# A feed-forward stage of seven products per group: the product with the fourth weight quarter goes second, and is kept in SBUF

## The chip, the cores and the metric

The kernel runs on one core of a Trainium2 chip. The metric is the device time of one execution, in microseconds (us). Inside the core, TensorE (PE) multiplies matrices and writes PSUM; VectorE (DVE) and ScalarE (ACT) work elementwise; GpSimd (POOL) does a few small operations and issues DMAs that add to their target; SyncE (SP) issues all other DMAs of weights. Every engine works through its own instructions in a fixed order, and waits for the others through semaphores.

## The reference

Two layers of an encoder trunk, 512 tokens by 1024 features, float32. A layer is an attention and pooling stage, with a residual, and then a gated feed-forward stage with a residual:

```python
hn = rmsnorm(x, norm2_g[i])
gate, up = jnp.split(hn @ w_ffn_in[i], 2, axis=-1)
x = x + (jax.nn.silu(gate) * up) @ w_ffn_out[i]
```

`w_ffn_in` is 1024 x 5632, `w_ffn_out` is 2816 x 1024. The change is in the feed-forward stage, and in a few buffers that it borrows from the attention stage.

## The kernel before

**Splitting.** TensorE multiplies in a format with fewer bits than float32, so each float32 operand is split into a high part (`whi`, `xh`, `fh`) and a low part (`wlo`, `xl`, `fl`), and a product is three matmuls (`three`, L279): high by high, high by low, low by high. A weight piece is 128 x 1024 floats, 0.5 MB. It is loaded by SP into one of seven buffers `raw` (`loaded`, L219) and split into one of six pairs of buffers `whi` and `wlo` (`parts`, L229), in one of two ways. Without a piece number ACT casts the high part and DVE subtracts for the low part (L212). With a piece number ACT casts the high part (L236), ACT writes its negative into `wlo` (L237), and POOL issues a DMA that loads the same piece from HBM once more and adds it to `wlo` (L238): this is called the correction below.

**Feed-forward.** The 22 blocks of 128 hidden features are worked in six parts. Two blocks, the odd group (`odd_group`, L820), are multiplied in the plain way. The other twenty form five groups of four (`GROUPS`, L40), and in each group the product of tokens by weights is computed in the way of Strassen and Winograd: the input is cut in four quarters (two halves of the tokens, two halves of the 1024 features) and so is the weight (two halves of the features, two pairs of hidden blocks), and seven products of quarters or of sums of quarters take the place of eight. They are numbered 1 to 7. Products 1, 2 and 4 use weight quarters as loaded; 5, 6, 7 and 3 use sums and differences that DVE makes in place in the `raw` buffers (L887, L893, L894, L907). The sums of the input are made once in a layer (`Sets`, L712; `sums`, `third`, `fourth`).

A product is 24 matmuls of 128 x 128 by 128 x 512 (two weight pieces, two token blocks of 128, two feature blocks, three matmuls each) into two PSUM banks, one for each token block. The banks come from three small pools: `sc` (2 banks, `a`), `tr` (2 banks, `c`) and `mm` (3 banks, `b`, shared with other work).

The order of the products is written out by hand:

```python
PRODUCTS = (1, 5, 6, 2, 7, 4, 3)
LOADS = {1: ((0, 0),), 5: ((1, 0), (1, 4)), 2: ((0, 4),), 4: ((1, 4),)}
```

`LOADS` says which quarters (pair of blocks, first feature block) are loaded ahead of a product, each as two pieces. The fourth quarter, (1, 4), is loaded twice in a group: for the first sum (product 5) and again for product 4 as a plain quarter. The first sum is built in the buffer of the fourth quarter, the second sum in the buffer of the first quarter, which so stays held until product 3.

After product 1 its result is copied to SBUF (`x1`, L925), and product 2 goes on adding to the same banks; the sum goes to `put`. Product 7 adds to the banks of product 6, once DVE has read them for `x2` (L933). After 7, DVE makes `x1` (L943) and `c22` (L945), reading banks `b` and `c`; after 4 it makes the last sum (L954); product 3 adds to banks `c` (L957) and ends `x2` (L959).

**Hidden blocks.** `put` (L797) applies the gate (ACT, L804, and DVE, L805) and turns the block by tokens into one by features: DVE transposes 32 x 32 squares (L316), SP stores the block to HBM (`away`, L317) and loads it back in another order with four DMAs (`near`, L321). `back` (L813) then splits it into `fh` and `fl` (L212).

**Output units.** A unit (`out_unit`, L836) multiplies 128 output features with the hidden blocks of one group into a bank, in turn `oy` or one of `mm`, and DVE adds it to the residual (L707). Units of an earlier group are put between the products of a later one by the table `UNITS` (L43): the key is the group and the product after which they stand. The last eight pairs of units follow after the fifth group.

**What sets the order.** The order on PE is fixed as written (`in_turn`, L288, ties each chain of matmuls to the one before it). On the other engines and on SP's queue, a scheduler orders the instructions at compile time by their place in the program and by when it reckons them ready; at run time each engine keeps that order. `later` (L260) puts the second half of a turn further on in the program.

**Borrowed buffers.** `rotate` (L368) uses two small tiles `m1` and `m2`, with two buffers each. The head gains of the two layers have a tile each (`hg0`, `hg1`, L188), and the row of norms of a layer lies in the tile of the other layer (L482). The pool weights' two parts have a tile each (L651).

## Time and profile before

| what | value |
|---|---|
| three runs | 1403.54, 1403.58, 1405.05 us |
| median of the runs | 1403.58 us |
| the profiled execution | 1406.57 us |
| its span, first to last instruction | 1404.8 us |
| granted TensorE clock, mean | 0.996 |
| weight loads `raw<-in_wts` issued by SP | 264 of 512 KB, 4.6 us to landing (median) |
| corrections `wlo<-in_wts` issued by POOL | 64 of 512 KB, 7.9 us to landing (median) |

The profile comes from one execution, 3.0 us longer than the median of the runs. In a row of its timeline stand the start, the duration (or, for merged instructions, the whole stretch), the engine, the line, the operation with its target and sources, the shapes and the count; in square brackets the engine's idle time before it, and what ended that. "SPq" is SP's queue of DMA issues. In a row of a table by windows stand the window, its length, and for PE, weight loads, DVE, ACT and POOL the busy time with the number of instructions that touch the window; then the granted clock, the share of the 16 DMA engines' time that packets took, and GB/s. Busy matmuls overlap, so that PE's busy time can be full while it runs slowly; the number of matmuls in a window of given length shows that.

### The profile page before, as it was taken

The numbers are of one execution on the slowest core, as the hardware profiler recorded it, in microseconds if no ns is written. First come the engines' busy times: TensorE is split into PE (matmuls) and PEld (weight loads), VectorE is DVE, ScalarE is ACT, GpSimd is POOL, SyncE is SP. The second block draws the span as 40 slices with busy tenths as digits, with TensorE's granted clock in tenths as the row PEclk, the third lists the DMA queues.
The fourth block names the chain that finished last, engine by engine and source line by source line (L and its number), as shares of the span: only waits on it lengthen the run. The fifth ranks groups of instructions, "written<-read, shape, count | busy, mean of one in ns | idle before, by whom it ended". The sixth has DMA issues, their size and how long they took to land.

```text
span 1404.8 us, 18608 instructions
## 1 busy us (share of the span) xinstructions
PE 1380.7 (98%) x6242; PEld 1140.8 (81%) x6242; DVE 1046.0 (74%) x1979; ACT 694.7 (49%) x1301; POOL 117.7 (8%) x139
## 2 busy tenths in 40 slices
PE   9999999999999999999999999999999989999999
PEld 7888888887887788888878787888878867888887
DVE  7779788686877768587667886877868767686772
ACT  7445343444765455545345543445457644555450
POOL 1010000000111000100010101001001100001000
PEclk9999999999999999999999999999999999999999
DMA  8334454455496876878434345534534967869661
GB/s 304 106 128 121 142 150 142 130 146 145 91 253 156 257 208 195 219 194 264 128 110 136 108 143 182 160 122 127 174 106 96 271 162 236 232 174 242 193 178 60
DMA packets 143663, 235.00 MB, mean 167 GB/s; under 512 B 41168, under 2 KB 88784, under 8 KB 143568
## 3 DMA queue, kind: packets, MB, share of 16 engines
q1 hardware_dynamic: 133056, 198.14, 43.2%
q0 software_dynamic: 9216, 33.56, 13.5%
q10 hardware_dynamic: 1296, 2.12, 0.5%
q8 instruction: 49, 0.80, 0.2%
q14 instruction: 46, 0.38, 0.1%
HBM read 204.53 MB, written 29.23 MB: 166 GB/s over the span
## 4 chain that ended last, share of the span: by engine, by line
PE 84%; DMA 6%; DVE 5%; issue 2%; ACT 1%; POOL 1%; SPq 1%; ACTq 0%; POOLq 0%; DVEq 0%
PE mm L301 12%; PE mm L302 12%; PE mm L303 12%; PE mm L283 6%; PE mm L284 6%; PE mm L282 6%; PE sc L283 3%; PE sc L282 3%; PE sc L284 3%; PE oy L282 3%; PE oy L284 3%; PE oy L283 3%; PE tr L282 2%; PE tr L283 2%; PE tr L284 2%; DMA away<-near 2%
## 5 line engine op out<-in xcount | busy, mean ns | idle before, releaser
L212 ACT CAST whi<-raw 128x1024 fp32r<-128x1024 f32 (+1 forms) x241 | 251.1, 1048 | 207.6 <-PE mm L283 53.5
L212 DVE TENSOR_TENSOR wlo<-raw,whi 128x1024 fp32r<-128x1024 f32 (+1 forms) x241 | 291.3, 1213 | 62.5 <-ACT whi L212 61.5
L301 PE MATMUL mm<-whi,xh 128*128 128x512 f32 x480 | 188.7, 393 | 1.0 <-DVE qn L601 1.0
L303 PE MATMUL mm<-whi,xl 128*128 128x512 f32 x480 | 187.2, 390 | 0.0
L302 PE MATMUL mm<-wlo,xh 128*128 128x512 f32 x480 | 187.1, 390 | 0.0
L303 PEld LDWEIGHTS mm<-whi,xl 128*128 128x128 f32 x480 | 90.1, 188 | 19.1
L301 PEld LDWEIGHTS mm<-whi,xh 128*128 128x128 f32 x480 | 90.2, 188 | 18.6 <-PE mm L303 1.4
L302 PEld LDWEIGHTS mm<-wlo,xh 128*128 128x128 f32 x480 | 90.2, 188 | 17.4
L238 POOL DMA_DIRECT2D wlo<-in_wts x64 | 56.1, 876 | 565.6 <-ACT wlo L237 390.3
L346 POOL TENSOR_TENSOR r<-r,mhalf 128x1 f32<-128x1 f32 (+1 forms) x64 | 56.7, 887 | 525.8 <-DVE r L345 422.8
L301 PE MATMUL mm<-xh,whi 128*128 128x512 f32 x256 | 99.8, 390 | 0.0
L302 PE MATMUL mm<-xl,whi 128*128 128x512 f32 x256 | 99.7, 390 | 0.0
L303 PE MATMUL mm<-xh,wlo 128*128 128x512 f32 x256 | 99.6, 389 | 0.0
L283 PE MATMUL sc<-wlo,xh 128*128 128x512 f32 x240 | 94.2, 393 | 5.5 <-DMA wlo<-in_wts 5.5
L707 DVE TENSOR_TENSOR res<-mm,res 128x512 f32<-128x512 f32 x96 | 65.2, 681 | 39.8 <-PE mm L284 33.6
L282 PE MATMUL sc<-whi,xh 128*128 128x512 f32 x240 | 94.1, 392 | 0.0
L284 PE MATMUL sc<-whi,xl 128*128 128x512 f32 x240 | 94.1, 392 | 0.0
L237 ACT ACTIVATE wlo<-raw 128x1024 fp32r<-128x1024 f32 x64 | 67.4, 1057 | 23.1 <-PE mm L283 14.0
L282 PE MATMUL oy<-fh,whi 128*128 128x512 f32 (+1 forms) x180 | 69.9, 388 | 6.1 <-DVE res L707 6.1
L284 PE MATMUL oy<-fh,wlo 128*128 128x512 f32 (+1 forms) x180 | 69.8, 388 | 0.0
L283 PE MATMUL oy<-fl,whi 128*128 128x512 f32 (+1 forms) x180 | 69.7, 387 | 0.0
L282 PE MATMUL mm<-fh,whi 128*128 128x512 f32 (+1 forms) x176 | 68.5, 389 | 0.0
(239 smaller groups left out, 3100.7 us busy)
## 6 DMA issues: line engine op xcount, KB each, us to landing
raw<-in_wts SPq DMA_DIRECT2D x264, 512.0 KB, 4.6
wlo<-in_wts POOLq DMA_DIRECT2D x64, 512.0 KB, 7.9
away<-near SPq DMA_DIRECT2D x72, 256.0 KB, 2.6
near<-away SPq DMA_DIRECT2D x288, 64.0 KB, 2.1
away<-near SPq DMA_DIRECT2D x28, 128.0 KB, 1.7
near<-away SPq DMA_DIRECT2D x112, 32.0 KB, 2.6
res<-in_x_t SPq DMA_DIRECT2D x4, 512.0 KB, 6.8
pwr<-in_pool_w ACTq DMA_DIRECT2D x8, 256.0 KB, 2.7
```

The costliest lines, as they stand in the source:

```text
L212: return nc.scalar.copy(hi, src), nc.vector.tensor_sub(lo, src, hi.bitcast(F32))
L237: made[0] = nc.scalar.activation(lo, raw, AF.Copy, scale=-1.0)
L238: nc.gpsimd.dma_start(lo.rearrange("p a b -> p (a b)"), wts[piece_no], accum_op=ALU.add)
L282: nc.tensor.matmul(acc, lhsT=ah, rhs=bh, start=start, stop=False, **check)
L283: nc.tensor.matmul(acc, lhsT=ah, rhs=bl, start=False, stop=False, **check)
L284: last = nc.tensor.matmul(acc, lhsT=al, rhs=bh, start=False, stop=stop, **check)
L301: nc.tensor.matmul(acc, lhsT=ah, rhs=bh, start=i == 0, stop=False)
L302: nc.tensor.matmul(acc, lhsT=ah, rhs=bl, start=False, stop=False)
L303: last = nc.tensor.matmul(acc, lhsT=al, rhs=bh, start=False, stop=i == n - 1)
L346: nc.gpsimd.tensor_tensor(r, r, mhalf[:, :width], op=ALU.pow)
L707: return nc.vector.tensor_add(res[d][:, cs], acc, res[d][:, cs])
```

## The change

Product 4 moves from the sixth place to the second. The fourth quarter is loaded once: its two pieces are split for product 4 by casts and correction, and the same `raw` buffers then serve the first sum. Product 4's result is copied from PSUM into SBUF by ACT (`x4`) and added, in SBUF, to `x1` after product 7, where both halves of the second pair of blocks are then put. The second sum has tiles of its own, under the tags `pw` and `hg`, where the pool weights' two parts now share one tile, and where one tile holds the head gains and the row of norms, for both layers in turn. `m1` and `m2` become parts of one tile with one buffer, which also holds one half of `x4`. `UNITS` is written for the new order; the units keep their places in the sequence. `third` is called after product 5 instead of 6, and `fourth` before the groups instead of at product 7.

```diff
-PRODUCTS = (1, 5, 6, 2, 7, 4, 3)
-LOADS = {1: ((0, 0),), 5: ((1, 0), (1, 4)), 2: ((0, 4),), 4: ((1, 4),)}
-UNITS = {(0, 7): [(-1, 0)], (0, 4): [(-1, 1)], (0, 3): [(-1, 2)], (1, 1): [(-1, 3)], (1, 4): [(0, 0)], (1, 3): [(0, 1)],
-         (2, 1): [(0, 2)], (2, 5): [(0, 3)], (2, 4): [(1, 0)], (2, 3): [(1, 1)],
-         (3, 1): [(1, 2)], (3, 5): [(1, 3)], (3, 4): [(2, 0)], (3, 3): [(2, 1)],
-         (4, 1): [(2, 2)], (4, 5): [(2, 3)]}
+PRODUCTS = (1, 4, 5, 6, 2, 7, 3)
+LOADS = {1: (0, 0), 4: (1, 4), 5: (1, 0), 2: (0, 4)}
+UNITS = {(0, 2): [(-1, 0)], (0, 7): [(-1, 1)], (0, 3): [(-1, 2)], (1, 1): [(-1, 3)],
+         (1, 7): [(0, 0)], (1, 3): [(0, 1)], (2, 1): [(0, 2)], (2, 4): [(0, 3)],
+         (2, 7): [(1, 0)], (2, 3): [(1, 1)], (3, 1): [(1, 2)], (3, 4): [(1, 3)],
+         (3, 7): [(2, 0)], (3, 3): [(2, 1)], (4, 1): [(2, 2)], (4, 4): [(2, 3)]}
...
-    for tag in ("m1", "m2"):
-        sb.tile([P, 4, ROT], F32, name=tag, tag=tag, bufs=2)
+    sb.tile([P, 4, 4, ROT], F32, name="m12", tag="m12")
...
-        g = sb.tile([P, 2 * QK + VD], F32, name="hg", tag=f"hg{layer}")
-        qkg[layer], sg[layer] = g[:, :2 * QK], g[:, 2 * QK:]
+        g = sb.tile([P, 2, S], F32, name="hg", tag="hg")
+        qkg[layer], sg[layer], rms_rows[layer] = g[:, 0, :2 * QK], g[:, 0, 2 * QK:], g[:, 1, :]
...
-            hi = sb.tile([P, 2, VD], F32R, name="pwh", tag="pwh")
-            lo = sb.tile([P, 2, VD], F32R, name="pwl", tag="pwl")
+            both = sb.tile([P, 2, 2, VD], F32R, name="pw", tag="pw")
+            hi, lo = both[:, 0], both[:, 1]
...
                 if not k:
                     x.sums()
+            x.fourth()
             token_stats(False)
```

The new `prepare` and the new loop over the products:

```python
def prepare(n):
    got = [loaded() for _ in range(2 if n in LOADS else 0)]
    if got:
        raws[n] = [raw for raw, _ in got]
    if n in (1, 4, 2):
        sets[n] = [parts(*r) for r in got]
        return
    sets[n] = []
    for h in range(2):
        if n == 5:
            made_of = raws[4][h]
            with ExitStack() if g else tc.issue_after(x.added.ins):
                nc.vector.tensor_add(made_of, raws[5][h], made_of)
        elif n == 6:
            made_of = sb.tile([P, 2, 512], F32, name="s2", tag=("pw", "hg")[h])
            nc.vector.tensor_sub(made_of, raws[4][h], raws[1][h])
            nc.vector.tensor_sub(raws[5][h], raws[1][h], raws[5][h])
            raws.setdefault(6, []).append(made_of)
        elif n == 7:
            made_of = raws[5][h]
        else:
            made_of = raws[2][h]
            nc.vector.tensor_sub(made_of, made_of, raws[6][h])
        sets[n].append(parts(made_of))
...
for n in PRODUCTS:
    prepare(n)
    if n in (4, 6):
        b = [mm_ps() for _ in range(2)]
    bank = {1: a, 2: a, 4: b, 6: b, 7: b, 5: c, 3: c}[n]
    multiply(n, bank, n in (1, 4, 5, 6))
    for t in range(2):
        if n == 1:
            x1[t] = temp("ta", 2)
            nc.scalar.copy(x1[t], a[t])
        elif n == 4:
            x4[t] = temp(*(("qn", 3), ("m12",))[t])
            nc.scalar.copy(x4[t], b[t])
        elif n == 6:
            x2[t] = temp("qn", 3)
            nc.vector.tensor_add(x2[t], b[t], x1[t])
        elif n == 2:
            to[0].put(0, t, a[t][:, :VD], a[t][:, VD:])
        elif n == 7:
            nc.vector.tensor_add(x1[t], b[t], x1[t])
            c22 = temp(("ah", "al")[t])
            nc.vector.tensor_add(c22, c[t], x1[t])
            to[1].put(1, t, c22[:, :VD], c22[:, VD:])
        elif n == 3:
            nc.vector.tensor_add(x2[t], c[t], x2[t])
            to[0].put(1, t, x2[t][:, :VD], x2[t][:, VD:])
    if n == 7:
        for t in range(2):
            nc.vector.tensor_add(x4[t], x4[t], x1[t])
            to[1].put(0, t, x4[t][:, :VD], x4[t][:, VD:])
    if n == 5 and not g:
        x.third()
```

More of the change, by code (lines that the diff above doesn't have):

```diff
@@ L109, in weight_plan @@
             for n in PRODUCTS:
-                for q in LOADS.get(n, ()):
-                    for h in range(2):
-                        quarter(f0, *q, h)
+                for h in range(2 if n in LOADS else 0):
+                    quarter(f0, *LOADS[n], h)
                 for source, i in UNITS.get((g, n), ()):
@@ L370, in rotate @@
         ca = cos_t[:, t, :].unsqueeze(1).broadcast_to([P, 4, ROT])
-        m1 = sb.tile([P, 4, ROT], F32, name="m1", tag="m1", bufs=2)
-        m2 = sb.tile([P, 4, ROT], F32, name="m2", tag="m2", bufs=2)
+        both = sb.tile([P, 4, 4, ROT], F32, name="m12", tag="m12")
+        m1, m2 = both[:, 0], both[:, 1]
         nc.vector.tensor_mul(m1, qn[:, :, :ROT], ca)
@@ L474, in trunk_kernel @@
     head_gains(0)
-    rms_rows = {}
     def spread_rms(layer):
@@ L481, in spread_rms @@
             transpose(row[:, token(t)], stats[0][:, 1, t:t + 1].broadcast_to([P, P]))
-        rms_rows[layer] = sb.tile([P, S], F32, name="rr", tag=f"hg{1 - layer}")
         nc.scalar.copy(rms_rows[layer], row)
@@ new lines, in prepare @@
+                got = [loaded() for _ in range(2 if n in LOADS else 0)]
[3 more added lines that the diff above has]
+                    sets[n] = [parts(*r) for r in got]
+                    return
+                sets[n] = []
+                for h in range(2):
+                    if n == 5:
+                        made_of = raws[4][h]
+                        with ExitStack() if g else tc.issue_after(x.added.ins):
+                            nc.vector.tensor_add(made_of, raws[5][h], made_of)
+                    elif n == 6:
+                        made_of = sb.tile([P, 2, 512], F32, name="s2", tag=("pw", "hg")[h])
+                        nc.vector.tensor_sub(made_of, raws[4][h], raws[1][h])
+                        nc.vector.tensor_sub(raws[5][h], raws[1][h], raws[5][h])
+                        raws.setdefault(6, []).append(made_of)
+                    elif n == 7:
+                        made_of = raws[5][h]
+                    else:
+                        made_of = raws[2][h]
+                        nc.vector.tensor_sub(made_of, made_of, raws[6][h])
+                    sets[n].append(parts(made_of))
@@ L916, in multiply @@
                                 start and not h)
-            x1, x2, c22 = [None] * 2, [None] * 2, [None] * 2
+            x1, x2, x4 = [None] * 2, [None] * 2, [None] * 2
             for n in PRODUCTS:
                 prepare(n)
-                if n == 1:
-                    multiply(1, a)
-                    for t in range(2):
+                if n in (4, 6):
+                    b = [mm_ps() for _ in range(2)]
+                bank = {1: a, 2: a, 4: b, 6: b, 7: b, 5: c, 3: c}[n]
+                multiply(n, bank, n in (1, 4, 5, 6))
+                for t in range(2):
+                    if n == 1:
@@ L932, in group @@
                         x2[t] = temp("qn", 3)
                         nc.vector.tensor_add(x2[t], b[t], x1[t])
-                    if not g:
-                        x.third()
-                elif n == 2:
-                    multiply(2, a, False)
-                    for t in range(2):
+                    elif n == 2:
                         to[0].put(0, t, a[t][:, :VD], a[t][:, VD:])
-                elif n == 7:
-                    multiply(7, b, False)
-                    for t in range(2):
+                    elif n == 7:
@@ L943, in group @@
                         nc.vector.tensor_add(x1[t], b[t], x1[t])
-                        c22[t] = temp(("ah", "al")[t])
-                        nc.vector.tensor_add(c22[t], c[t], x1[t])
-                    if not g:
-                        x.fourth()
-                    for t in range(2):
-                        to[1].put(1, t, c22[t][:, :VD], c22[t][:, VD:])
-                elif n == 4:
-                    a = [s_ps() for _ in range(2)]
-                    multiply(4, a)
-                    for t in range(2):
-                        nc.vector.tensor_add(x1[t], a[t], x1[t])
-                        to[1].put(0, t, x1[t][:, :VD], x1[t][:, VD:])
-                elif n == 3:
-                    multiply(3, c, False)
-                    for t in range(2):
+                        c22 = temp(("ah", "al")[t])
@@ L959, in group @@
+                        nc.vector.tensor_add(c22, c[t], x1[t])
+                        to[1].put(1, t, c22[:, :VD], c22[:, VD:])
+                    elif n == 3:
                         nc.vector.tensor_add(x2[t], c[t], x2[t])
                         to[0].put(1, t, x2[t][:, :VD], x2[t][:, VD:])
+                if n == 7:
+                    for t in range(2):
+                        nc.vector.tensor_add(x4[t], x4[t], x1[t])
+                        to[1].put(0, t, x4[t][:, :VD], x4[t][:, VD:])
@@ L961, in group @@
+                if n == 5 and not g:
+                    x.third()
                 for source, i in UNITS.get((g, n), ()):
```

41 lines of the change are left out of this document (3 added, 38 removed).

## The prediction

> **What bounds the kernel now.** The page first: its head and its rows for the engines and the DMA queues.
>
> ```profile
> span 1404.8 us, 18608 instructions
> PE 1380.7 (98%) x6242; PEld 1140.8 (81%) x6242; DVE 1046.0 (74%) x1979; ACT 694.7 (49%) x1301; POOL 117.7 (8%) x139
> ...
> q1 hardware_dynamic: 133056, 198.14, 43.2%
> q0 software_dynamic: 9216, 33.56, 13.5%
> ```
>
> TensorE is the bound, and the change leaves each of its 6242 matmuls in place. Only time in which PE stands still or runs slowly can be won. The PE waits, by cause (total, times, longest):
>
> ```profile
> PE oy L282 <- DVE res L707: 6.1, 3, 2.2
> PE sc L283 <- DMA wlo<-in_wts: 5.5, 3, 2.0
> ```
>
> Both are feed-forward lines: L707 empties the bank `oy` of an output unit, and `wlo` from `in_wts` is the correction that POOL's DMA adds to a weight (L238). PE's timeline holds all six:
>
> ```profile
> 437.90 0.50 PE L282 MATMUL oy<-fh,whi 128*128 128x512 f32 x1 [2.16 <-DVE res L707]
> 458.60 0.47 PE L283 MATMUL sc<-wlo,xh 128*128 128x512 f32 x1 [2.05 <-DMA wlo<-in_wts]
> 1136.52 0.50 PE L282 MATMUL oy<-fh,whi 128*128 128x512 f32 x1 [2.04 <-DVE res L707]
> 1152.19 0.47 PE L283 MATMUL sc<-wlo,xh 128*128 128x512 f32 x1 [1.53 <-DMA wlo<-in_wts]
> 1157.08 0.47 PE L283 MATMUL sc<-wlo,xh 128*128 128x512 f32 x1 [1.88 <-DMA wlo<-in_wts]
> 1194.40 0.47 PE L282 MATMUL oy<-fh,whi 128*128 128x512 f32 x1 [1.93 <-DVE res L707]
> ```
>
> Together 11.59 us idle, all in the second group of a layer or at the third group's first unit. The whole loss shows when those stretches are set beside the undisturbed ones after them (windows: length, PE busy and matmuls, ..., granted clock, DMA share, GB/s):
>
> ```profile
> 430.00:490.00 60.00, 55.79 (x231) 44.97 (x230) 45.05 (x57) 32.39 (x41) 5.22 (x6) 0.94 0.73 203
> 490.00:550.00 60.00, 60.00 (x266) 49.71 (x265) 43.90 (x56) 31.93 (x40) 5.21 (x6) 1.00 0.77 214
> ...
> 1128.00:1200.00 72.00, 64.62 (x282) 52.27 (x281) 53.31 (x68) 36.40 (x47) 5.22 (x6) 1.00 0.67 191
> 1200.00:1272.00 72.00, 72.00 (x319) 59.63 (x318) 51.38 (x64) 38.13 (x45) 6.95 (x8) 1.00 0.78 215
> ```
>
> 60 us hold 265 intervals, 0.2265 us a matmul. 35 are missing in layer 0 (7.9 us) and 37 in layer 1 (8.4 us): **16.3 us** lost, 11.6 of it idle. Most of the rest is clock, in layer 0:
>
> ```profile
> 438.00:442.00 4.00, 4.00 (x12) 3.15 (x13) 3.97 (x5) 1.75 (x3) 0.00 (x0) 0.64 0.40 94
> ```
>
> Right after the 2.16 us stop the granted clock was 0.64 for 4 us (4 x 0.36 = 1.4 us). Over the 60 us it was 0.94 in layer 0, some 3 us lost, and 1.00 in layer 1. The Trainium skill, "TensorE: Matmul & The Clock Gate", section "Why this matters for your kernels", asks only that no gap passes about 3 us; by that rule these stops would cost no clock, and the saving below would be 11.6 us and the restarts. The row above speaks against it.
>
> **Why these stops.** The first one backwards (ACT, then DVE, then SP's queue):
>
> ```profile
> 431.51 0.62 ACT L212 CAST fh<-near 128x512 fp32r<-128x512 f32 x1 [7.47 <-DMA near<-away]
> ```
> ```profile
> 432.16 0.69 DVE L212 TENSOR_TENSOR fl<-near,fh 128x512 fp32r<-128x512 f32 x1 [6.41 <-ACT fh L212]
> ...
> 437.16 0.68 DVE L707 TENSOR_TENSOR res<-oy,res 128x512 f32<-128x512 f32 x1
> ```
> ```profile
> 418.40 0.38 SPq L317 DMA_DIRECT2D away<-near  x1
> ...
> 423.81 2.66 SPq L321 DMA_DIRECT2D near<-away  x4
> ```
>
> A hidden block, turned through HBM, left at 418.40 and was back only at 431.5. ACT and DVE, both in order, held still for it, and the emptying of `oy` stood behind. The turn was slow because the DMA engines were full (windows; the last two numbers are DMA share and GB/s):
>
> ```profile
> 372.00:392.00 20.00, 20.00 (x94) 16.67 (x93) 15.45 (x26) 11.27 (x16) 1.97 (x2) 1.00 0.27 84
> 392.00:428.00 36.00, 36.00 (x160) 29.80 (x160) 25.34 (x34) 19.60 (x25) 4.35 (x5) 1.00 1.02 268
> ...
> 490.00:526.00 36.00, 36.00 (x160) 29.84 (x159) 23.25 (x27) 18.89 (x23) 3.49 (x4) 1.00 0.77 210
> ```
>
> The second stop, at 458.60, follows from the raw buffers (SP's waits, then DVE, SP, POOL):
>
> ```profile
> SPq L224 <- DVE raw L894: 50.3, 8, 19.3
> ```
> ```profile
> 442.48 1.22 DVE L894 TENSOR_TENSOR raw<-raw 128x1024 f32<-128x1024 f32 x1
> ```
> ```profile
> 443.76 17.68 SPq L224 DMA_DIRECT2D raw<-in_wts  x8
> ```
> ```profile
> 449.51 0.88 POOL L238 DMA_DIRECT2D wlo<-in_wts  x1 [1.03 <-ACT wlo L237]
> ```
>
> All seven raw buffers were held until L894, which DVE reached late for the reason above; product 2's second piece was loaded at 443.76, corrected from 449.51, and came in at 458.5.
>
> **The change, part by part.**
>
> *Two loads fewer in a group*, 20 of 0.52 MB. By the q1 row (607 us for 198.14 MB) one takes 1.6 us of all 16 engines; a correction, by the q0 row (190 us for 64), 3.0 us.
>
> *Buffers come free sooner.* Before, product 6 frees the two buffers of the first sum, and six stay held until 7 and 3: the pieces of 1 (as second sum), of 5 and of 2. After, the second sum has its own tiles, 6 frees the pieces of both 1 and 4, and four stay. So I expect that the output piece, the next one and a piece of the next group load before 392, where the share is 0.27, and that product 4's two corrections leave there too, instead of at 405:
>
> ```profile
> 390.41 0.93 POOL L238 DMA_DIRECT2D wlo<-in_wts  x1 [5.19 <-ACT wlo L237]
> ...
> 405.08 1.89 POOL L238 DMA_DIRECT2D wlo<-in_wts  x2 [11.43 <-ACT wlo L237]
> ```
>
> Out of the stretch 392 to 428 go 2 x 1.6 (dropped) + 3 x 1.6 (earlier) + 2 x 3.0 = 14 us; back come the next group's two corrections for product 4, 6 us. 36.7 - 8 = 29 us of 36: share 0.8, about that of 490 to 526, where nothing stops. I take all six stops as gone; the ends are none (0) and all (16.3 us).
>
> *Product 2 now has its weight slots from product 4*, with 5 and 6 between, as it had 1's slots with 5 and 6 between in the first group. First use there and the landing times:
>
> ```profile
> 400.45 0.39 PE L283 MATMUL sc<-wlo,xh 128*128 128x512 f32 x1
> ```
> ```profile
> DMA to landing us min/median/max: 5.4/7.9/10.8
> ```
> ```profile
> L925 ACT COPY cta<-sc 128x512 f32<-128x512 f32 x20 | 11.4, 586 | 5.4 <-PE sc L284 5.3
> ```
>
> That was 10.0 us from issue to use, without a stop. Afterwards two more copies (product 4 into SBUF, 0.59 each) stand on ACT before the second piece's casts; I work out 11.8 and 10.7 us of lead. The median fits; the largest misses the second by 0.1. Taken as 0; the price if the lead is used up is a rival below.
>
> *The copies* add 20 x 0.59 = 11.7 us to ACT (49% busy), beside PE; product 6 needs their `mm` banks one product, 5.4 us, later. The final add reads SBUF instead of PSUM: one add for one add. 0, or, if ACT is held as at 431.51, 2 us in a group.
>
> *Product 3 moves up behind 7.* It accumulates on bank `c`, which the add into `c22` must have read. In groups 1 to 4 a unit stands between; in the fifth none does, where now product 4 (5.4 us) does (DVE, then PE):
>
> ```profile
> 647.46 1.28 DVE L943 TENSOR_TENSOR cta<-mm,cta 128x512 f32<-128x512 f32 x2
> 648.66 0.68 DVE L945 TENSOR_TENSOR cah<-tr,cta 128x512 f32<-128x512 f32 x1
> ```
> ```profile
> 647.53 0.39 PE L284 MATMUL mm<-whi,xrl 128*128 128x512 f32 x1
> 647.75 0.39 PE L282 MATMUL sc<-whi,xh 128*128 128x512 f32 x1
> ```
>
> Product 3 would start at 647.75, and `c` is read at 649.34: **a new stop** of 1.6 us, 1.85 with restart, once in each layer: 3.7 us. It is 0.2 if DVE adds straight away in order, 2.9 if one more 1.2 us weight split goes first; 0.4 to 5.8 for both. I take the row as it stands. Behind this matmul stands all the rest of the layer on PE, so the stop counts in full.
>
> *Merged tiles.* `m1`/`m2` in one single buffer: all on DVE, in order, 0. The second layer's gains share a tile with the sums, and so can load only when the last group has let go, not here:
>
> ```profile
> 337.48 0.38 SPq L190 DMA_DIRECT2D hg<-in_rows  x1
> ```
>
> It would wait on SP, with raw loads behind it, until the fifth group's product 3 is prepared. The last eight pairs of output units, 43 us of PE at 24 matmuls each, hide that: 0. Without them the load's own time would show, once.
>
> *What else is moved past.* Product 4's two loads go ahead of 5's on SP, its four casts ahead on ACT, its corrections ahead of the odd group's statistics on POOL. Those statistics wait for the odd group's end, the casts for weight slots that come free halfway through it. `third` moves up behind 5; its splits are first needed by 7. 0 for all, hidden by the odd group's matmuls; a late correction there would hold the statistics, and with them every later `put`.
>
> **Sum**, against the profiled execution (1406.57 us, span 1404.8): -16.3 + 3.7 = -12.6, 1394.0. It lies 3.0 us over the median of the runs. Taken off the median, 1391.0; if those runs had no fall of the clock in layer 0 (some 3 of the 16.3 us), 1394. I say **1393**.
>
> **The rivals.**
> - *Half stays.* The turns come back sooner but still hold ACT somewhere; seven buffers still run out at product 6. For: ACT waits for a turn in other places too. 1403.58 - 8.2 + 3.7 = 1399.1.
> - *It does not do what it says*: the freed buffers only pull later loads into the same full stretch, and what is won is given back: around 1403.6.
> - *Transfers hidden anyway.* The stops stay, since ACT waits for a turn whose own steps set its time; the new one comes: 1407.3. The Trainium skill, "Perfetto Trace Analysis", section "Identifying the Most-Contended Engine", would have the busiest engine improved first, and that is not DMA. Against: share 1.02 just where the turn took 13 us.
> - *Slower: product 2's correction comes late.* ACT, held by a turn as at 431.51 just ahead of product 2's casts, uses up the lead: 7.5 + 7.9 - 11.8 = 3.6 us, in the first two groups of both layers, 14.4 us, with restarts (1) and two falls of the clock (3): 1391.0 + 18.4 = 1409.4. It decides once those four stops pass 3.2 us each (12.6 / 4). Against: product 2 stands ahead of those turns in the program.
>
> **How the numbers follow.** Forecast 0.55, half 0.20, given back 0.08, hidden 0.08, late 0.09. A measurement of this kernel tells about 0.2% (2.8 us) from no change. Faster: 0.55 and four fifths of half, 0.71. Slower: late and most of hidden, 0.16. Same: 0.13. Range: low is 1391.0 with the small end of the new stop (0.4), 1387.7; high takes in what is given back, 1404, and leaves out the two slower cases.
>
> **What would show it.** Right: no PE wait on L707 or on `wlo` in the first three groups; share under 0.9 between 392 and 428; no ACT wait over 3 us for a turn there; the second group's product 2 loaded before it starts product 4; a PE stop of 1 to 2 us before `tr` in the fifth group. Wrong: `wlo` waits in product 2 of the first two groups (late), DMA share still 1 (given back), ACT holds as long at a lower share (hidden), or waits outside the feed-forward stage.

## The result, and the profile after

| | median | runs | profiled execution | its span |
|---|---|---|---|---|
| before | 1404.32 us | 1403.54 to 1405.45, 4 runs | 1406.57 us | 1404.8 us |
| after | 1394.62 us | 1393.37 to 1395.41, 4 runs | 1394.02 us | 1392.2 us |

The ratio is 0.9929, with a 95% interval of 0.9912 to 0.9947: 9.7 us less by the medians, 12.6 us less between the two spans. The two differ because the profiled execution of before lay 2.3 us above its median, and that of after 0.6 us below.

The page of after, its head, PE's row and the queue of plain loads:

```profile
span 1392.2 us, 18593 instructions
...
PE 1375.2 (99%) x6242; PEld 1138.3 (82%) x6242; DVE 1045.5 (75%) x1979; ACT 703.3 (51%) x1321; POOL 117.7 (8%) x139
...
q1 hardware_dynamic: 130176, 187.65, 42.0%
```

The matmuls are the same 6242, the queue of plain loads moves 10.5 MB less (20 x 0.52), and ACT has 20 instructions more. Of the feed-forward waits of PE only one kind is left (waits: total, times, longest), and the timeline shows where:

```profile
PE tr L280 <- DVE cah L928: 3.1, 2, 1.6
```
```profile
648.47 0.47 PE L280 MATMUL tr<-whi,xh 128*128 128x512 f32 x1 [1.57 <-DVE cah L928]
...
1339.39 0.47 PE L280 MATMUL tr<-whi,xh 128*128 128x512 f32 x1 [1.58 <-DVE cah L928]
```

That is product 3 of the fifth group, which waits until DVE has read bank `c`. The six old stops are gone. By windows (length, then the busy times of PE, weight loads, DVE, ACT and POOL, granted clock, DMA share, GB/s):

```profile
372.00:392.00 20.00, 20.00 (x94) 16.68 (x93) 15.06 (x25) 10.88 (x18) 2.37 (x3) 1.00 0.76 186
392.00:428.00 36.00, 36.00 (x160) 29.82 (x159) 24.66 (x34) 22.93 (x30) 4.16 (x5) 1.00 0.77 193
430.00:490.00 60.00, 60.00 (x266) 49.69 (x266) 49.10 (x64) 35.13 (x46) 5.37 (x7) 1.00 0.85 222
1128.00:1200.00 72.00, 72.00 (x319) 59.70 (x318) 54.75 (x67) 41.89 (x54) 6.94 (x8) 1.00 0.76 206
```

The stretch 430 to 490 holds 266 matmuls where before held 231, and 1128 to 1200 holds 319 where before held 282: the 35 and 37 that were missing are back, 72 x 0.2265 = 16.3 us. And the DMA work has moved: 372 to 392 went from a share of 0.27 to 0.76, 392 to 428 from 1.02 to 0.77. With that the first halves of the turns land sooner. SP, which sends the second half of a turn once the first has landed, waited for that so long in all (before, then after: us, times, longest):

```profile
SPq L321 <- DMA away<-near: 180.5, 69, 7.6
```
```profile
SPq L319 <- DMA away<-near: 82.0, 55, 5.0
```

ACT, which had stood 7.47 us for the block put after product 7, at 431.51, now stands 1.64 us for that block (SP's queue, where it leaves, then ACT):

```profile
426.17 1.92 SPq L315 DMA_DIRECT2D away<-near  x2
```
```profile
438.88 0.62 ACT L210 CAST fh<-near 128x512 fp32r<-128x512 f32 x1 [1.64 <-DMA near<-away]
```

The turn of that block is not shorter. Before, it left at 418.40 and its last part landed at 431.41, 13.0 us later; now it leaves at 426.17 and lands at 438.78, 12.6 us later. What became shorter is ACT's wait, since its split stands at another place in the order. What that does is worked out below.

The new price is read at the fifth group. 25 us hold 112 matmuls in before (635 to 660); after has 104 there, 8 x 0.2265 = 1.8 us lost in each layer. So 16.3 - 3.6 = 12.7 us should have gone between the two spans, and 12.6 went.

### The profile page after: what moved, and what is told of

It is laid out like the page before. It is cut to its first block, busy times and chain, and to the rows that moved or that the text cites. A ratio compares the mean times of both kernels' runs of the same rounds, so it can differ in the third digit from the quotient of the medians.

```text
span 1392.2 us, 18593 instructions
## 1 busy us (share of the span) xinstructions
PE 1375.2 (99%) x6242; PEld 1138.3 (82%) x6242; DVE 1045.5 (75%) x1979; ACT 703.3 (51%) x1321; POOL 117.7 (8%) x139
## 4 chain that ended last, share of the span: by engine, by line
PE 89%; DVE 6%; issue 1%; POOL 1%; DMA 1%; ACT 1%; SPq 0%; DVEq 0%; POOLq 0%; ACTq 0%
PE mm L299 11%; PE mm L300 11%; PE mm L301 11%; PE mm L281 8%; PE mm L282 8%; PE mm L280 8%; PE tr L280 3%; PE tr L281 3%; PE tr L282 3%; PE oy L281 3%; PE oy L280 3%; PE oy L282 3%; PE sc L280 3%; PE sc L281 3%; PE sc L282 3%
## 5 line engine op out<-in xcount | busy, mean ns | idle before, releaser
L210 ACT CAST whi<-raw 128x1024 fp32r<-128x1024 f32 (+1 forms) x221 | 230.2, 1047 | 175.7 <-PE mm L300 42.0
L210 DVE TENSOR_TENSOR wlo<-raw,whi 128x1024 fp32r<-128x1024 f32 (+1 forms) x221 | 267.0, 1212 | 63.1 <-ACT whi L210 62.2
L234 ACT CAST whi<-raw 128x1024 fp32r<-128x1024 f32 x64 | 66.6, 1040 | 18.3 <-issue 17.7
L282 PE MATMUL mm<-fh,wlo 128*128 128x512 f32 (+1 forms) x176 | 68.1, 387 | 0.0
L281 PE MATMUL mm<-fl,whi 128*128 128x512 f32 (+1 forms) x176 | 68.1, 387 | 0.0
```

Source lines behind the costliest of these rows:

```text
L210: return nc.scalar.copy(hi, src), nc.vector.tensor_sub(lo, src, hi.bitcast(F32))
L234: nc.scalar.copy(hi, raw)
L281: nc.tensor.matmul(acc, lhsT=ah, rhs=bl, start=False, stop=False, **check)
L282: last = nc.tensor.matmul(acc, lhsT=al, rhs=bh, start=False, stop=stop, **check)
```

## The experiments

The result leaves open which part did it. The change does three things at once that could cure the stops: it **moves product 4** (its two corrections leave at 371.57 and 375.18 and not at 405, and the units and `put`s around it move too), it **loads two pieces fewer**, and it gives the **second sum own tiles**. The first four runs ask for each, and for the new stop. "Loss" below is what the feed-forward stage of one profile lost on PE against an unbroken stream of matmuls 0.2267 us apart, in its first and second layer. After loses 1.9 + 1.9 us by this count.

**The new stop.** One entry of `UNITS`: the last pair of output units that stands between products of the fifth group goes from behind product 4 to behind product 7.

```diff
-         (3, 7): [(2, 0)], (3, 3): [(2, 1)], (4, 1): [(2, 2)], (4, 4): [(2, 3)]}
+         (3, 7): [(2, 0)], (3, 3): [(2, 1)], (4, 1): [(2, 2)], (4, 7): [(2, 3)]}
```

> The kernel after, with one output unit of the fifth group moved from behind product 4 to behind product 7. Theory (the add into c22 holds product 3 up because nothing stands between 7 and 3 in the fifth group): both PE waits on L928 (1.57 and 1.58 us) go with their restarts, about 3.5 us shorter than the kernel after, 0.987 of the kernel before. Rival (the wait only moves: product 6 now stands one product behind 4, and its banks wait for ACT's copies of product 4): a PE wait of 1 to 2 us before product 6 in the fifth group, no gain, 0.993.

Measured: 1390.92 us (1389.87 to 1391.43, 6 runs), ratio to before 0.9904 [0.9887, 0.9922], 3.7 us under the changed kernel's median (in another session of runs, with before 0.9 us higher there). The fifth group's window now has all its matmuls:

```profile
635.00:660.00 25.00, 25.00 (x112) 20.71 (x111) 23.06 (x37) 12.15 (x17) 0.00 (x0) 1.00 0.62 200
1325.00:1350.00 25.00, 25.00 (x112) 20.72 (x111) 23.15 (x35) 12.24 (x17) 0.00 (x0) 1.00 0.40 128
```

Loss 0.1 + 0.1 us. So the new stop costs what it shows, and nothing comes in its place. (The 0.987 of the expectation does not follow from its own 3.5 us, which give 0.990.) By the span of the profile this version, with 1389.1 us, is shorter than both kernels.

**The second load given back.** The changed kernel, with quarter (1, 4) loaded again for product 5.

```diff
-LOADS = {1: (0, 0), 4: (1, 4), 5: (1, 0), 2: (0, 4)}
+LOADS = {1: ((0, 0),), 4: ((1, 4),), 5: ((1, 0), (1, 4)), 2: ((0, 4),)}
...
+                if n == 5:
+                    raws[4] = [raw for raw, _ in got[2:]]
```

> The kernel after, but the fourth quarter is loaded a second time for product 5, into buffers of its own; order, own tiles of the second sum and everything else as after. Theory that the number of loads counts: the DMA share between 392 and 428 us goes up by about 3 us of 36 and the buffers fill earlier, so that some of the six stops come back, 3 to 8 us longer than after. Rival (the order and the buffers that come free do it, the loads are hidden): no stop comes back, within 1 us of after.

Measured: 1396.12 us (1393.8 to 1396.46), ratio 0.9939 [0.9918, 0.996]. Loss 2.2 + 1.9 us; the only stops are the two new ones. The stretch 392 to 428 stays relieved:

```profile
392.00:428.00 36.00, 36.00 (x161) 29.81 (x160) 24.98 (x34) 22.94 (x30) 4.41 (x5) 1.00 0.74 184
```

Twenty loads of 0.52 MB more cost nothing that can be told. With the second sum in its own tiles, the dropped loads are not needed for the gain.

**The second sum in place.** The changed kernel, with the second sum made in the buffers of product 1's pieces, as before.

```diff
-                        made_of = sb.tile([P, 2, 512], F32, name="s2", tag=("pw", "hg")[h])
-                        nc.vector.tensor_sub(made_of, raws[4][h], raws[1][h])
-                        nc.vector.tensor_sub(raws[5][h], raws[1][h], raws[5][h])
+                        made_of = raws[1][h]
+                        nc.vector.tensor_sub(raws[5][h], made_of, raws[5][h])
+                        nc.vector.tensor_sub(made_of, raws[4][h], made_of)
```

> The kernel after, but the second sum is made in place in the first quarter's buffers, which so stay held until product 3, as before. Theory that buffers coming free sooner count: loads wait longer on SP, and the wlo waits in product 2 of the second group come back, 2 to 3.4 us in each layer, while the waits on the oy bank stay away; 4 to 7 us longer than after. Rival (order and load count do it): no stop, within 1 us of after.

Measured: 1395.27 us (1394.47 to 1396.09), ratio 0.9936 [0.9916, 0.9956]. Loss 2.4 + 2.4 us: beside the new stops there are two of 0.20 and 0.30 us on `wlo`. So, with the loads dropped, the own tiles aren't needed either.

**Before, once more.** The kernel before, unchanged, in another execution.

> The kernel before, profiled once more. Theory: the six feed-forward stops are there again at the same places with the same lengths within 0.3 us, since the order of every engine is fixed; whether the clock falls after the stops of layer 0 is chance, so that the profiled time lies anywhere from 1402 to 1407 us. Rival: the stops differ from one execution to the next, and a part of the difference between the two kernels' profiles is chance.

Measured: 1406.37 us, one run. The stops are there again, but with other lengths, and some elsewhere. From PE's timeline:

```profile
437.15 0.50 PE L282 MATMUL oy<-fh,whi 128*128 128x512 f32 x1 [0.28 <-DVE res L707]
452.49 0.47 PE L283 MATMUL sc<-wlo,xh 128*128 128x512 f32 x1 [1.18 <-DMA wlo<-in_wts]
457.75 0.47 PE L283 MATMUL sc<-wlo,xh 128*128 128x512 f32 x1 [2.29 <-DMA wlo<-in_wts]
...
1135.53 0.50 PE L282 MATMUL oy<-fh,whi 128*128 128x512 f32 x1 [0.98 <-DVE res L707]
```

The stop of 2.16 us on `oy` is now 0.28, and a new one of 1.18 on `wlo` stands beside it. There are nine stops in place of six, 4.6 us in the first layer and 7.9 us in the second. Loss 5.7 + 9.4 = 15.1 us, against 8.1 + 8.4 in the first profile (16.3 in all by the prediction's count). No fall of the clock is in layer 0 here (430 to 490 at 1.00). So one stop of one profile is not a fixed price; in these two executions the sum over both layers is nearly one.

After these four, the place of product 4 seemed to be all of it. The next four were made to test that against the two other parts taken together, and against transfer time as such.

**The place alone.** Both edits above at once: the load given back and the sum in place.

> The changed kernel with both of its other parts undone: quarter (1,4) is loaded a second time for product 5, and the second sum is made in the buffers of product 1's pieces again, so that four buffers more are held or moved than in the changed kernel. Only the place of product 4 (with the units and the adds that go with it) is left. Theory 'the place': product 4's pieces and corrections take their DMA time before 392 us, where the engines stood at a share of 0.27, and that is enough: 1394 to 1397 us, no stop of PE on oy or wlo over 0.5 us, share in 392 to 428 under 0.9. Rival 'either of the other two': fewer loads and own tiles each do the same job, so one alone could be taken away, but not both: 1400 to 1404 us, with oy and wlo stops of 1 to 2 us back in the second group and share near 1.

Measured: 1403.04 us (1401.15 to 1404.28, 10 runs), ratio 0.9986 [0.9976, 0.9995]. The theory falls: with the place alone nearly the whole gain is lost. The main stops that came back are those on `wlo` in product 2 of the second group, and not those on `oy` there:

```profile
455.08 0.47 PE L282 MATMUL sc<-wlo,xh 128*128 128x512 f32 x1 [0.36 <-DMA wlo<-in_wts]
460.05 0.47 PE L282 MATMUL sc<-wlo,xh 128*128 128x512 f32 x1 [1.97 <-DMA wlo<-in_wts]
...
1158.23 0.47 PE L282 MATMUL sc<-wlo,xh 128*128 128x512 f32 x1 [1.80 <-DMA wlo<-in_wts]
```

Later in layer 0 stand one more of 1.36 us on `wlo` (582.40) and one of 0.41 on `oy` (561.53). The stretch 392 to 428 has a share of 0.83 here: relieved, as in after. Loss 7.3 + 6.5 us, of which 3.6 are the new stop: of the old 16.5 us some 10 are left.

**Own tiles alone.** The kernel before, in its order and with all its loads, with the second sum in tiles of its own.

```diff
+                        s2 = sb.tile([P, 2, 512], F32, name="s2", tag=("pw", "hg")[h])
+                        nc.vector.tensor_sub(s2, s1, r11)
...
-                        nc.vector.tensor_sub(r11, s1, r11)
-                        sets[6].append(parts(r11))
+                        raws.setdefault(6, []).append(s2)
+                        sets[6].append(parts(s2))
```

> The kernel before, with the second sum in tiles of its own (and the tile of the gains merged for them), in the old order and with all 24 loads: two buffers come free at product 6. Theory 'the place': corrections for product 4 still leave at 405, so the stops on oy stay, and of the stops on wlo at most those go that followed from the lack of buffers (3 to 5 us in both layers): 1399 to 1404 us. Rival 'the buffers': more buffers pull the loads ahead by themselves: share in 372 to 392 over 0.6, no stop left, and 1388 to 1392 us, since the new stop ahead of product 3 doesn't come.

Measured: 1398.79 us (1397.93 to 1401.44), ratio 0.9963 [0.9949, 0.9977]. Nearly the mirror image: of the stops on `wlo` in product 2 of the second group only one of 0.16 us is left (three small ones of 0.46, 0.62 and 0.16 in all), and stops ahead of output units remain:

```profile
490.01 0.47 PE L282 MATMUL oy<-fh,whi 128*128 128x512 f32 x1 [1.20 <-DVE res L705]
...
1124.55 0.47 PE L282 MATMUL oy<-fh,whi 128*128 128x512 f32 x1 [1.96 <-ACT th L802]
...
1187.79 0.47 PE L282 MATMUL oy<-fh,whi 128*128 128x512 f32 x1 [1.72 <-DVE res L705]
```

They are not all the old ones. The stop of 2.16 us at 437.90 is gone and its fellow of 2.04 in the second layer is down to 0.25, while the first two shown stand where the first profile of before had none. So this relief reaches the stops on `oy` in part. The share in 392 to 428 is 0.95. Loss 1.5 + 7.2 us.

**Product 4's corrections taken out, in the old order.** The kernel before; product 4's low parts come from DVE, which takes ten corrections in each layer off POOL's queue (64 become 44; the expectation's ten are those of one layer). With them twenty negations go from ACT, and twenty subtractions come to DVE.

```diff
-                    sets[4] = [parts(*r) for r in got[0]]
+                    sets[4] = [parts(r) for r, _ in got[0]]
```

> The kernel before, with product 4's weights split by DVE (1.2 us a piece more there) in place of POOL's accumulating DMA: ten corrections fewer, two of which (3.0 us of the 16 engines each) stood in 392 to 428. Theory 'the place' in the form that a full stretch of DMA makes the stops: share there falls from 1.0 to about 0.85, the turn at 418 comes back sooner, the stops on oy go, and product 2's corrections land sooner: 1390 to 1397 us. Rival 'in-order engines, not DMA': what held DVE and ACT is the order of the program, and DVE has 1.2 us more for each piece: 1401 to 1408 us with stops as before.

Measured: 1393.69 us (1392.25 to 1395.67), ratio 0.9923 [0.9907, 0.9939]: the whole gain of the change, from one line and without any of its parts. No stop on `oy` is left. One on `wlo` stays in each layer. With it, as in before, goes a correction that leaves 7.5 us before PE comes to it (POOL, then PE):

```profile
445.47 0.86 POOL L238 DMA_DIRECT2D wlo<-in_wts  x1 [1.02 <-ACT wlo L237]
```
```profile
454.52 0.47 PE L283 MATMUL sc<-wlo,xh 128*128 128x512 f32 x1 [1.35 <-DMA wlo<-in_wts]
...
1146.80 0.47 PE L283 MATMUL sc<-wlo,xh 128*128 128x512 f32 x1 [1.52 <-DMA wlo<-in_wts]
```

Loss 1.7 + 1.8 us. So there are two kinds of stop with two causes, and the traces show what each is made of.

*On `oy`, in the second group.* In the old order, DVE empties the bank (L707) behind the split of the block that was put after product 7. In the two executions of before this stop comes four times, and each time PE's matmul starts 6.39 us after ACT takes that block up: 431.51 and 437.90, 1130.13 and 1136.52 in the first execution, 430.76 and 437.15, 1129.14 and 1135.53 in the second. The ACT row of the first pair is in the prediction, those of the others are:

```profile
1130.13 0.62 ACT L212 CAST fh<-near 128x512 fp32r<-128x512 f32 x1 [6.76 <-DMA near<-away]
```
```profile
430.76 0.62 ACT L212 CAST fh<-near 128x512 fp32r<-128x512 f32 x1 [5.65 <-DMA near<-away]
```
```profile
1129.14 0.62 ACT L212 CAST fh<-near 128x512 fp32r<-128x512 f32 x1 [4.01 <-DMA near<-away]
```

The stop is what is left of these 6.39 us when PE comes to the bank. With the corrections out, ACT is free for the block at 424.20, as before (424.04), but the block lands 4.0 us sooner: 427.46 + 6.39 = 433.85, and PE comes only at 436.46. So there it is the time of the transfers that cures, and not the lighter load of ACT. With own tiles alone it is 430.02 + 6.39 = 436.41, and PE comes at 436.95: no stop, by half a microsecond. In the changed order the cure is another one: DVE empties that bank at 430.95, ahead of the split of the block after product 7, and the late block no longer matters. The block whose split stands ahead now is that after product 2, and its turn did become shorter, 6.9 us (414.79 to 421.67) against 11.7 (408.67 to 420.36).

*On `wlo`, in product 2 of the second group.* The stop is what the correction of the second piece takes to land, less its lead, the time from its issue until PE would come to it. In layer 0:

| run | second sum | fourth quarter | lead, us | to land, us | stop, us |
|---|---|---|---|---|---|
| after | own tiles | loaded once | 8.6 | 6.2 | 0 |
| second load given back | own tiles | loaded twice | 6.7 | 6.3 | 0 |
| second sum in place | in place | loaded once | 8.7 | 8.9 | 0.20 |
| place alone | in place | loaded twice | 6.7 | 8.7 | 1.97 |
| own tiles alone | own tiles | loaded twice | 6.4 | 6.0 | 0 |
| corrections out | in place | loaded twice | 7.5 | 8.9 | 1.35 |
| before | in place | loaded twice | 6.9 | 9.0 | 2.05 |

The issues of after and of the place alone, from POOL's rows:

```profile
450.68 0.86 POOL L236 DMA_DIRECT2D wlo<-in_wts  x1 [1.02 <-ACT wlo L235]
```
```profile
451.20 0.86 POOL L237 DMA_DIRECT2D wlo<-in_wts  x1 [1.02 <-ACT wlo L236]
```

Layer 1 shows the same within 0.4 us. In the new order the dropped load buys 2 us of lead, and in either order the own tiles take 2.4 to 3 us off the landing. One of the two is enough there, and without both the stop is back. Where the sum is made in place, two raw loads that had waited for product 3's sums leave on either side of this correction (448.49 and 450.39 beside 449.51 in before); with own tiles none leaves within the 2 us after it (452.70 after 450.68). That may be why it lands late; no run isolates it.

**Transfers added on SP's queue.** The changed kernel with four idle copies of 0.52 MB, HBM to HBM, behind product 4's loads in each group.

```diff
+                if n == 4:
+                    for _, i in got * 2:
+                        copy = hbm.tile([P, 1024], F32, name="idle", tag="idle", bufs=8)
+                        nc.sync.dma_start(copy, wts[i])
```

> The changed kernel with four idle copies of 0.52 MB from HBM to HBM put on SP's queue in each group right behind product 4's two loads; nothing reads them. They add 2.1 MB read and as much written to each group, in the stretch that the change filled (372 to 392), and push SP's next transfers back. Theory 'full DMA makes the stops': share near 1 in 372 to 428 and PE stops of 1 to 2 us on oy or wlo come back in the second group of both layers: 1398 to 1408 us. Rival 'the order of the engines alone': DMA time doesn't matter there, no stop but the two known ones of 1.57 us: 1394 to 1396 us.

Measured: 1400.72 us (1399.15 to 1402.72), and it tells nothing about the question. The view by line shows why: the copies wait for nothing, and all forty left in the first 250 us, ahead of the feed-forward stage.

```profile
L880 SPq DMA_DIRECT2D idle<-in_wts x40: 488/538/1005, 33.9 to 249.7; - x40
```

The feed-forward loss is 1.9 + 1.9 us as in after; the 5.2 us that the span grew by lie in front of it, in the attention stage of layer 0, where 21 MB more were read and as much written (one stop of 2.61 us at 73.98 among it).

**Both cures in the old order.** Own tiles and product 4 split by DVE, on the kernel before.

> The kernel before in its old order and with all 24 loads, with the two reliefs of the last runs together: product 4's weights split by DVE in place of ten accumulating DMAs (that alone took away the stops on oy and left one of 1.35 and 1.52 us on wlo), and the second sum in tiles of its own (that alone took away the stops on wlo in the second group and left those on oy). Theory 'two causes': the stops on oy come from the full DMA stretch, those on wlo from the lack of raw buffers, and each has its own cure: no feed-forward stop over 0.5 us, no new stop ahead of product 3 either, 1389.5 to 1392.5 us. Rival 'one cause, and the cures overlap': 1393 to 1396 us with a stop on wlo left.

Measured: 1391.55 us (1387.98 to 1393.83), ratio 0.9913 [0.9894, 0.9931]. Not one stop is left in either feed-forward stage, loss 0.1 + 0.1 us:

```profile
430.00:490.00 60.00, 60.00 (x267) 49.67 (x266) 53.26 (x67) 31.68 (x41) 3.49 (x4) 1.00 0.75 224
...
1128.00:1200.00 72.00, 72.00 (x319) 59.66 (x318) 56.18 (x69) 37.68 (x45) 5.25 (x6) 1.00 0.75 211
```

Two kinds of stop, each with its own cure, and the order of the products need not be touched for either.

**Transfers added in the right place.** The version of the first run (its move of a pair of units is meant by "unit (2,3)"), with six idle copies of 0.52 MB from SBUF to HBM on POOL's queue behind product 2's corrections in the first full group of each layer. They read a weight slot, so that they can't leave early.

```diff
+                    for k in range(6 if n == 2 and not g else 0):
+                        copy = hbm.tile([P, 1024], F32, name="idle", tag="idle", bufs=12)
+                        nc.gpsimd.dma_start(copy, sets[2][1][0].rearrange("p a b -> p (a b)").bitcast(F32))
```

> The changed kernel with the second half of unit (2,3) moved behind product 7 (1390.9 us, no stop in the feed-forward stage), and on POOL's queue six idle copies of 0.52 MB from SBUF to HBM behind product 2's corrections in the first full group of each layer, read by nothing; they read a weight slot, so they cannot leave earlier, about 399 us in layer 0. Theory 'a full DMA stretch makes the stops on oy': six times 1.3 to 3 us of the 16 engines bring the share in 392 to 428 from 0.77 to 0.95 or more, the turns of the hidden blocks come back late, ACT waits over 4 us for one, and stops of 1 to 2 us on oy come back in the second group of both layers: 1394 to 1402 us. Rival 'the order of the engines alone': no stop on oy, 1390 to 1392 us.

Measured: 1398.17 us (1397.37 to 1398.65), ratio 0.9962 [0.9948, 0.9976]. Stops came back on `wlo` in both layers, and on `oy` in the first layer alone, with a 7 us wait of ACT for a turned block ahead of it. ACT, then PE:

```profile
415.72 1.05 ACT L210 CAST whi<-raw 128x1024 fp32r<-128x1024 f32 x1 [3.56 <-DMA idle<-whi]
429.12 0.62 ACT L210 CAST fh<-near 128x512 fp32r<-128x512 f32 x1 [7.10 <-DMA near<-away]
```
```profile
437.24 0.50 PE L280 MATMUL oy<-fh,whi 128*128 128x512 f32 x1 [1.11 <-DVE res L703]
...
459.82 0.47 PE L281 MATMUL sc<-wlo,xh 128*128 128x512 f32 x1 [2.39 <-DMA wlo<-in_wts]
...
1151.34 0.77 PE L281 MATMUL sc<-wlo,xh 128*128 128x512 f32 x1 [2.22 <-DMA wlo<-in_wts]
```

It looks like a proof, but for the first ACT row: the copies held the weight slot, and ACT stood 3.56 us for it. That is a second possible cause, so the run was repeated with copies out of the second sum's tile, which holds nobody up, six of them and then three.

```diff
+                        with tc.issue_after(last[0].ins):
+                            nc.gpsimd.dma_start(copy, raws[6][1].rearrange("p a b -> p (a b)"))
```

> The last run again (six idle copies of 0.52 MB behind product 2's corrections in the first full group), but out of the tile of the second sum, which nothing overwrites before the next group, in place of a weight slot: there the copies held the slot, and ACT waited 3.6 us for it in layer 0, a second possible cause of what came back. Theory 'a full DMA stretch': it comes back all the same, share in 392 to 428 about 0.9, an ACT wait over 4 us for a hidden block near 429, feed-forward loss of 5 to 9 us in both layers together: 1395 to 1400 us. Rival 'the held slot': loss under 2 us, 1390 to 1393 us.

> The same with three copies in place of six. Theory 'a full DMA stretch', with a point from which it decides: half the added transfers leave the share at about 0.83, the value at which other kernels here ran without stops on oy: loss under 2 us, 1390 to 1393 us. Rival 'each transfer costs in proportion': half of what six cost, 2.5 to 4.5 us: 1393 to 1396 us.

Measured: 1390.59 us (1389.95 to 1390.82), ratio 0.9904 [0.9889, 0.9919] with six; 1389.32 us (1388.39 to 1390.83), ratio 0.9896 [0.988, 0.9913] with three. Against the first run's 0.9904 no difference can be told. Loss 0.6 + 0.7 us and 0.1 + 0.1 us. The same window with the slot held (first fence) and without it (second), six copies in both:

```profile
392.00:428.00 36.00, 36.00 (x160) 29.84 (x159) 20.42 (x26) 17.62 (x21) 6.80 (x10) 1.00 0.89 268
```
```profile
392.00:428.00 36.00, 36.00 (x161) 29.82 (x160) 22.81 (x31) 20.59 (x27) 6.81 (x10) 1.00 0.89 270
```

The share is equal to the digit, and one loses 8.8 us, the other 1.2. The **share over a stretch is not what decides**; this form of the theory falls. What differs is ACT and, through it, the order of events: the late cast let the raw load behind it go at 418.06, right ahead of the turn's reads at 418.48, instead of at 415.47.

```profile
418.06 0.33 SPq L222 DMA_DIRECT2D raw<-in_wts  x1
```
```profile
415.47 0.33 SPq L222 DMA_DIRECT2D raw<-in_wts  x1
```
```profile
424.90 0.62 ACT L210 CAST fh<-near 128x512 fp32r<-128x512 f32 x1 [2.58 <-DMA near<-away]
```

ACT then had the block at 424.90 and not at 429.12, though SP sent its reads in the same tenth of a microsecond.

ACT's longest wait for a turned block in the second group, in layer 0 between 420 and 445 us, stands here beside the stop ahead of the output unit at about 437 and the share in 392 to 428 (the runs left out stood 1.9 us or less and had no such stop):

| run | ACT's wait, us | stop on `oy`, us | DMA share |
|---|---|---|---|
| before | 7.47 | 2.16 | 1.02 |
| six copies, slot held | 7.10 | 1.11 | 0.89 |
| before again | 5.65 | 0.28 | 0.97 |
| place alone | 4.18 | 0 | 0.83 |
| own tiles alone | 4.13 | 0 | 0.95 |
| second load given back | 3.65 | 0 | 0.74 |
| both cures, old order | 3.30 | 0 | 0.84 |
| corrections out, old order | 3.26 | 0 | 0.91 |
| six copies, no slot held | 2.58 | 0 | 0.89 |
| after | 1.64 | 0 | 0.77 |

The share does not order the stops: there is none at 0.95 and 0.91, and one at 0.89. ACT's wait orders them in this layer, but it is not the measure either: in layer 1 before, again, stood 4.01 us and lost 0.98, and the run with the slot held stood 4.78 us and lost nothing on `oy`. What holds in both layers is when ACT takes the block up, against when PE comes to the bank. In the run with the slot held the block is the one after product 2, and the matmul starts 8.12 us after ACT takes it up (429.12 and 437.24; PE was there at 436.13). By the same 8.12 us the bank is ready at 1128.64 in its second layer, and PE comes at 1129.69: no stop.

## Why the prediction was right

- **The forecast** was 1393.0 us, by a step of -12.6 us from the profiled execution; that step was 12.6 between the spans, and the median came out at 1394.6. Between the medians the step was 9.7 us only. The time came out near the forecast because the step was taken off an execution that lay 2.3 us above before's median; taken off the median it would have given 1391.0. That much is luck, or the prediction's own alternative, that most runs of before lose less than the profiled one; no run splits the two.
- **The loss that goes**, 16.3 us by two pairs of windows, came back whole: 72 matmuls. But the prediction read its six stops as six prices. The second execution of before shows that they vary, 0.28 for 2.16; the sum is what held (15.1).
- **The clock**, some 3 us in layer 0, belongs to that execution and not to the kernel: the second one shows no fall there, and lost 5.7 us in that layer in place of 8.1. It stood longer in layer 1, 9.4 for 8.4, so that the whole differs little. The last section has more on the clock.
- **The new stop**, 1.6 us and 1.85 with restart: 1.57 and 1.58, 1.8 by the count of matmuls, and 3.7 us by taking it away. Right to a tenth, since it was read from two rows of before: when product 3 could start and when DVE has read its bank.
- **"Buffers come free sooner"** and the sum of DMA work that leaves 392 to 428 (share 0.8, found 0.77) were right as a description. As causes they were mixed up. *Two loads fewer* and *own tiles* were both given a part of the relief; each can be taken away without a loss that can be told (1396.1, 1395.3), but not both (1403.0). They do two things: one gives the correction of product 2 more lead, the other a shorter landing. And one sign of being right did not come: product 2 of the second group was not loaded before product 4. Its second piece left on SP at 441.50, and PE began product 4 at 440.02.
- **"The second stop follows from the first"** (DVE late at L894, hence the load at 443.76) is a step that failed. With the corrections out and no stop on `oy`, the whole chain came 4.04 us sooner: L894 at 438.44 for 442.48, the load at 439.72 for 443.76, the correction at 445.47 for 449.51. But PE, no longer stopped, came to the matmul 3.4 us sooner too, and 1.35 and 1.52 us stayed. The cause is the lead and the landing of that correction, 7.5 and 8.9 us there. That the change cures both kinds of stop is why the total was right.
- **"The DMA engines were full"** as the reason of the late turn is the other: half right. Taking out product 4's corrections, the transfers at 405, does bring the turn back 4.0 us sooner and cures the stops on `oy` (1393.7). But in the changed kernel the turn of the block after product 7 took 12.6 us for 13.0, at a share of 0.77 for 1.02. A lower share did not shorten it, as the rival "transfers hidden anyway" supposed. The stop went because the emptying of the bank no longer stands behind that block. And 3.1 MB of plain copies in the same stretch, at a share of 0.89, made no stop on `oy`.
- **Product 2's correction**, taken as 0 with a lead of 11.8 and 10.7 us: the corrections left at 395.17 and 397.95, and PE came to them at 407.61 and 410.33, 12.4 us both, with 6.2 us to land (median). Right, for the first group, which it was worked out for. The rival in which it comes late is real where ACT is held: in the run with the slot the second group's first correction left at 454.19, 3.1 us before PE came to it, and PE stood 2.39 us (2.22 in layer 1).
- **The rivals' times** were met by two of the runs, but not by the rivals' paths. "Half stays", 1399.1, counts 8.2 us won and 3.7 of the new stop; own tiles alone (1398.8) have no new stop and lose 8.7 us. "Given back", 1403.6, has the old stops return; the place alone (1403.0) loses some 10 us of old stops and 3.6 of the new one.
- **The rest at 0**: no wait on the merged tiles or on the copies came to PE. The second layer's gains did wait on SP, until 628.29, and nothing was late for it.

Left open: why six copies with the slot held delayed the turn's reads by 4 us and six without it did not. The raw load ahead of them is the only difference found; the collision itself was not isolated. Nor was why a correction lands in 6 us with own tiles and in 9 without, nor were the stops at the third group's first unit (1194.40 in before) and the new ones in the run with own tiles alone taken apart.

## What to carry to other kernels

Add up lost matmuls over whole stages rather than pricing single stops: in two executions the sum repeated within a tenth, a single stop didn't. Where several stops vanish with one change, undo its parts in pairs, not only one by one; two parts that each seem useless may stand in for each other. For a stop that ends with a late transfer, set its lead beside its time to land: a change can work on either, and two halves can each be enough. And when an in-order engine waits for a round trip through memory, look first at what stands behind that wait in its order, then at what was sent just ahead of it, and try the one line that takes that out of the way before rewriting an order: here it was worth as much as the whole change.

## What the runs showed of the hardware

A stop of some 2 us does not always cost clock. Stops of 2.29 us (before again, layer 0) and 2.39 us (six copies, slot held, layer 0) were followed by a granted clock of 1.00; the one of 2.22 us in layer 1 of that same run was followed by 0.57 for 4 us:

```profile
1151.00:1155.00 4.00, 3.66 (x9) 2.98 (x10) 3.06 (x4) 0.00 (x0) 0.00 (x0) 0.57 1.04 316
```

The length of the stop alone does not tell which. The rule quoted in the prediction from the Trainium skill, "TensorE: Matmul & The Clock Gate", section "Why this matters for your kernels", agrees with the first two and not with the last. The first profile of before is split in the same way: 2.05 us were followed by 0.70 (458 to 462), and 2.04 us by 1.00 (1136 to 1140).

And a full share is not a rate: in 392 to 428 before moved 268 GB/s at a share of 1.02, with accumulating corrections among the loads, and the run with six copies out of the sum's tile 270 GB/s at 0.89 (both rows are shown above and in the prediction).
